# SwiGLU's splits one or two products later, operand reads two products later, and no idle reads at the end

## The chip, the cores and the metric

The kernel runs on one core of a Trainium2 chip. The metric is the device time of one execution in microseconds (us). A core has five engines that run side by side, each its own list of instructions in order: PE (TensorE, the matmuls; PEld is its weight load), DVE (VectorE), ACT (ScalarE), POOL (GpSimd) and SP (SyncE), which in this kernel does nothing but issue DMAs. The kernel is written with a manual schedule: the order of the Python calls is the order on each engine, and semaphores are put between them where one needs another's result.

## The reference

One layer with 512 tokens of width 2048: an input projection, three token mixers, an output projection, and a SwiGLU feed-forward with residuals. Only the last line of the layer matters here:

```python
    x = x + mix @ w_out[l]
    h2 = _rms_norm(x, norm2_g[l])
    x = x + (jax.nn.silu(h2 @ w_gate[l]) * (h2 @ w_up[l])) @ w_down[l]
```

The feed-forward's inner width is 5632, that is 44 blocks of 128. All is float32 and has to stay accurate, so each operand of a matmul is split in a high part (a cast to fp32r) and a low part (the rest), and three products of the parts are added.

## The kernel before, in words

**Stages.** From 0 to 585 us the projections and mixers (not touched). From 585 to 1436 us the gate and up products, in groups `Wide` g = 0 to 21. From 1436 us on the down products: `Turned` t = 0 to 7 up to 1754 us, then `Down` t = 8 to 15. In the program's main loop (L1594 on) the three are one loop over g, with t = g - 22, so that t = -2 and t = -1 are the last two groups of the gate and up stage.

**A group.** Each group multiplies two by two blocks by a Strassen scheme with seven products, in the order `ORDER = (5, 1, 7, 6, 2, 4, 3)`. The group's weights come as raw tiles of 128x1024 named '11', '12', '21', '22' with a group (w6, d0) and a sub-index 0 or 1. Sums of raw tiles (L213, POOL) make the other operands, tiles named 's'. One product of `Wide` and `Turned` is two units, one unit uses one weight tile and is 12 matmuls of 128x512 (L1387). So a group has 14 units. A unit's weight tile is first split: ACT casts it to `wn` (L277) and to `wh` (L278), DVE subtracts to `wl` (L279). `next_unit` writes the split of the tile that comes two units later (`SPLIT_AHEAD`), and there are three buffers of `wh` and `wl`. `pump` (L257 to L264) issues the read of the next raw tile on SP as soon as, in program order, its buffer is free.

**Operands of the gate and up products.** They are kept split, as tiles `h` named by product and block, in a pool of 68 slots. Those of products 1 and 7 (`KEEP`) stay; those of the other five are written to DRAM (`hd`) and read again (`load_op`, L1590) for the half of the blocks that the next odd group needs: two groups in a row share a half. These reads are queued in `loads`, three a product (`LOADS`), and each goes on SP at the end of the next product.

**SwiGLU's results.** An odd group g finishes the pair (g-1, g): its results go through Silu (L1524) to DRAM (`zd`). They come back as tiles of the two blocks p = g-1 and p = g, `f{p}r` and `f{p}l` (`Pair.load`, L1303), the r tiles one product after the group's last, the l tiles four products after. From them POOL makes sums `f{p}ta` and `f{p}tb` (`sums1`, `sums2`, L1311 to L1318), and four pieces are split into the seven operands `a{q}_{p}` of the down products: `piece3` from r, `piece4` from l, `piece1` from ta, `piece2` from tb. A piece is a near cast on ACT (L1323), one or two casts on ACT (L1330), one or two subtractions on DVE (L1331), and a write to DRAM (`od`, L1245) for each operand. `PIECES_AT` says how many products later each step runs, for p even and p odd, in the order sums1, sums2, piece3, piece4, piece1, piece2.

**Operands of the down products.** `load_act` (L1585) reads the tiles `a` back from `od`, four blocks for each product of t = 0.

**Queues.** `later(n, ..., queue=extras)` puts a call at the end of the n-th product from now; `run(extras)` runs what is due at the end of each product. All DMAs stand in SP's one list in this order, so a read that waits for a free buffer holds up all that stand behind it.

Of the kernel before, what the change touches and what calls it, by code (L numbers as in the profile page):

```python
# [70 lines left out]
ORDER = (5, 1, 7, 6, 2, 4, 3)  # L71
# [6 lines left out]
J_SET = NJ // 2  # L78


KEEP = (1, 7)
LOADS = 3
PIECES_AT = ((5, 5, 4, 5, 6, 7), (6, 6, 5, 6, 8, 11))


BY = 4
# [42 lines left out]
def kernel(ctx: ExitStack, tc: tile.TileContext, xT, wi, wo, wgu, wd, cst_in, outT):  # L129
# [34 lines left out]
    units = [wi[0][:, :T], wi[0][:, T:]] + [wi[u] for u in range(1, 2 * N_IN)]  # L164
# [3 lines left out]
    entries, works = [], []  # L168

    sums = defaultdict(list)  # L170
    raws, held = {}, {}

    def take(buf, key, n=1024):
        assert buf not in held
        held[buf] = key
        if buf[0] == "x":
            raws[key] = (wide(int(buf[1]), f"w{key}"), n)
        else:
            raws[key] = (wp.tile([P, 1024], F32, name=f"w{key}", tag=f"raw{buf}", bufs=1), n)
        return raws[key][0]  # L180

    def drop(key):
        for buf in [b for b, k in held.items() if k == key]:
            held.pop(buf)
        return raws.pop(key)

    for u, unit in enumerate(units):
# [9 lines left out]
    def down_group(name, n, subs):  # L197

        u, many = len(works), len(subs)
        key = {(k, i): (k, name, i) for k in ("11", "12", "21", "22", "s") for i in range(many)}  # L200
        into = {}
        for ks in (("21", "22"), ("11",), ("12",)):
            for i in range(many):
                for k in ks:
                    entries.append((ring(k if k[0] == "2" else "1"), key[k, i], subs[i][k]))
        for i in range(many):
            into[i] = ring("s")

        def add(i, to, a, b, last=None):
            def go():  # L210
                out = raws[key[to, i]][0] if to == a else take(into[i], key[to, i], n)
                eng = nc.vector if name == "w0" and "12" not in (a, b) else nc.gpsimd
                eng.tensor_add(out[:, :n], raws[key[a, i]][0][:, :n], raws[key[b, i]][0][:, :n])  # L213
                if last:
                    drop(key[last, i])
            return go

        for i in range(many):
            at_sum = FIRST_SUMS_AT[i] if name == "w0" else SUMS_AT[many][i]
            for d, args in zip(at_sum, (("s", "21", "22"), ("21", "21", "11"), ("s", "s", "11", "11"),  # L220
                                        ("s", "s", "12"))):
                sums[u + d].append(add(i, *args))
        for k, last in (("s", False), ("11", False), ("21", True), ("s", False), ("12", True), ("22", True), ("s", True)):
            works.extend((key[k, i], last, None) for i in range(many))
# [6 lines left out]
    def set_of(g):  # L231
        return (g + 1) // 2 % 2
# [20 lines left out]
    at = {"entry": 0, "split": 0, "use": 0}  # L253

    def pump(limit):
        while at["entry"] < len(entries) and len(raws) < limit and entries[at["entry"]][0] not in held:
            buf, key, parts = entries[at["entry"]]  # L257
            (part,) = parts
            n = part.shape[-1] * (part.shape[1] if len(part.shape) == 3 else 1)
            t = take(buf, key, n)[:, :n]  # L260
            nc.sync.dma_start(t if len(part.shape) == 2 else t.rearrange("p (n c) -> p n c", n=part.shape[1]), part)
            at["entry"] += 1
# [20 lines left out]
    def split_in_steps(i):  # L283

        def cast():
            if at["split"] > min(i, len(units) - 1):
                return
            u = at["split"]
            at["split"] += 1
            t, n = drop(works[u][0])  # L290
            hi = wp.tile([P, 1024], F32R, name=f"wh{u}", tag="hi", bufs=SPLIT_BUFS)
            lo = wp.tile([P, 1024], F32R, name=f"wl{u}", tag="lo", bufs=SPLIT_BUFS)
            nc.scalar.copy(hi, t)  # L293
            ticks.after(1, low, u, t, hi, lo)

        def low(u, t, hi, lo):
            nc.vector.tensor_sub(lo, t, hi.bitcast(F32))  # L297
            splits[u] = (hi, lo)

        ticks.after(1, cast)  # L300

    def sums_now():
        for fn in sums.pop(at["use"], ()):
            fn()

    def next_unit(ahead=SPLIT_AHEAD, split=split_up_to):
        sums_now()
        u = at["use"]
        at["use"] += 1
        split(u + ahead)  # L310
        pump(RAW_EARLY if u < 20 else RAW_BUFS + N_WIDE)
        return splits.pop(u)
# [724 lines left out]
    for name in PROJ[HEAD4:]:  # L1037
        kind, what, j = name[0], name[1], name[2:]
# [39 lines left out]
    ops, opening_ops = {}, {}  # L1078
# [160 lines left out]
    evacs, extras = [], []  # L1239
    flip = [1]  # L1240

    def run(queue):

        for fn, *args in queue.pop(0) if queue else ():
            fn(*args)  # L1245

    def later(n, fn, *args, queue=evacs):
        while len(queue) <= n:
            queue.append([])
        queue[n].append((fn, *args))  # L1250
# [103 lines left out]
    def load_y(t):  # L1354
        if N_TURNED <= t < N_DOWN:
            for n in (t - N_TURNED, t - N_TURNED + 8):
                y[n], x2[n] = slot(f"y{n}"), slot(f"x2_{n}")
                d = yd[n - n % 2]
                nc.sync.dma_start(y[n].rearrange("p (k a x) -> p k a x", k=2, a=4),
                                  bass.AP(tensor=d.tensor, offset=d.offset + n % 2 * P * 64,  # L1360
                                          ap=[[64, P], [P * T, 2], [32 * T, 4], [1, 64]]))
                nc.sync.dma_start(x2[n], x2d[n])
# [94 lines left out]
    class Wide(Turned):  # L1457
# [8 lines left out]
        def done(self, q, banks):  # L1466
# [38 lines left out]
            if q == 3:  # L1505
                for k, at in enumerate(PIECES_AT):
                    one = Pair(self.g - 1 + k)
# [84 lines left out]
    loads = []  # L1592
# [3 lines left out]
    for g in range(G_STEPS + N_DOWN):  # L1596
        t = g - G_STEPS
        turned = 0 <= t < N_TURNED
        if t < 0:
            blk = Wide(g, blk)  # L1600
        else:
            blk = (Turned if turned else Down)(t)
        for i, q in enumerate(ORDER):
            sums_now()
            run(evacs)
            for sub in range(BY // 2 if t < N_TURNED else 1):
                w = next_unit()
                if t < 0:
                    first = J_SET * set_of(g) + 2 * sub
                    blk.multiply(i, sub, w, [ops[q, j] for j in range(first, first + 2)])  # L1610
                    if ticks.due:
                        ticks.tick()
                elif turned:
                    first = BY * (t // 2) + 2 * sub
                    blk.multiply(i, sub, w, [acts[q, j] for j in range(first, first + 2)])
                else:
                    blk.multiply(q, w, [acts[q, j] for j in range(TURNED, NP)])
            if g == 0 and i in (2, 5):
                (norm2a if i == 2 else norm2b)()

            if t < 0 and (g % 2 == 0 or t == -1):
                for j in range(J_SET * set_of(g), J_SET * (set_of(g) + 1)):
                    if q not in KEEP or t >= -2:
                        ops.pop((q, j))
                        if 0 < g and t < -1:
                            loads.append((load_op, q, J_SET * (1 - set_of(g)) + j % J_SET))
                    if t == -1:
                        loads.append((load_act, q, [j % J_SET]))
                if g == 0 and i == 0:
                    held.pop("x1"), held.pop("x3")  # L1630
                    opening_ops.clear()
            elif turned and t % 2:
                first = BY * (t // 2)
                for j in range(first, first + BY):
                    acts.pop((q, j))
                first += BY
                if first < TURNED:
                    later(1, load_act, q, range(first, first + BY), queue=extras)
            for fn, *args in loads[:LOADS]:
                later(1, fn, *args, queue=extras)  # L1640
            del loads[:LOADS]
            if N_TURNED - 2 <= t < N_TURNED:
                n = 4 - (t % 2 == 0)
                for q2, j in rest[:n]:
                    later(1 if t % 2 else 0, load_act, q2, [j], queue=extras)
                del rest[:n]
            if i == (5 if turned else 3):
                load_y(t + 1)
            run(extras)
# [85 lines left out]
```

## Time and profile before

| what | us |
|---|---|
| median of 3 runs | 1877.76 (1877.58 to 1878.87) |
| profiled execution, device time | 1877.44 |
| its span, first to last instruction | 1875.2 |
| PE busy in the span | 1853.6 |
| DVE busy | 1533.1 |
| ACT busy | 1366.0 |
| POOL busy | 1082.9 |

By stage, from the view of busy time in stretches:

| stretch, us | PE | DVE | ACT | POOL | DMA share | GB/s |
|---|---|---|---|---|---|---|
| 0 to 585 | 583.11 | 479.30 | 301.06 | 221.49 | 0.46 | 147 |
| 585 to 1436 | 843.46 | 721.05 | 739.24 | 551.35 | 0.78 | 246 |
| 1436 to 1754 | 309.15 | 232.99 | 243.80 | 219.41 | 0.76 | 252 |
| 1754 to 1875 | 117.92 | 99.73 | 81.96 | 90.68 | 0.71 | 206 |

The page's other parts are: the span in 40 slices with PE's granted clock and the DMA load, the DMA queue (one queue of SP moves nearly everything, 398.89 of 400.60 MB), the chain of work that ended last (93% PE, 4% DMA, 1% ACT), the costliest groups of instructions, and the DMA issues, among them 208 reads of `h` (256 KB each, 5.4 us from issue to landing in the median), 154 writes of operands to `od` and 154 reads of them (5.8 us each). A row of the timeline has its start, its duration, engine, line, operation, output and inputs, and in brackets the engine's idle time ahead of it with what ended that.

### The profile page before, as it was taken

What the parts mean: (1) busy time and instruction counts of PE and PEld (TensorE: products, weight loads), DVE (VectorE), ACT (ScalarE), POOL (GpSimd) and SP (SyncE); (2) the same over time, 40 slices, a digit from 0 to 9 for tenths busy, and PEclk for the clock granted to TensorE, in tenths of its full rate; (3) what the DMA queues carried; (4) which work ended last, traced back from release to release, by engine and by line L of the source; (5) the groups of instructions that cost most, each with busy time, mean ns of one, the idle gap of its engine ahead of it and who ended that gap; (6) DMA issues with size and microseconds to landing.
All of it is one profiled execution on the core that took longest, in us unless ns stands there. A gap on an engine that the chain in (4) does not pass through costs nothing.

```text
span 1875.2 us, 26746 instructions
## 1 busy us (share of the span) xinstructions
PE 1853.6 (99%) x8548; PEld 1539.9 (82%) x8548; DVE 1533.1 (82%) x2318; ACT 1366.0 (73%) x1956; POOL 1082.9 (58%) x681
## 2 busy tenths in 40 slices
PE   9999999999999999999999999999999899999999
PEld 7888888888888888887888878888788688888888
DVE  7688899997579779798798887988878577778887
ACT  6235565555366789898898988988889787777675
POOL 5013444462253557576675676666766667766786
PEclk9999999999999999999999999999999899999999
DMA  7334333443397477879778797787889785578984
GB/s 260 135 100 120 99 98 98 117 129 111 118 326 243 128 201 243 265 235 291 227 238 271 230 297 235 234 271 225 286 258 323 229 306 190 192 256 286 308 238 124
DMA packets 319708, 400.60 MB, mean 214 GB/s; under 512 B 81104, under 2 KB 210256, under 8 KB 319568
## 3 DMA queue, kind: packets, MB, share of 16 engines
q1 hardware_dynamic: 319424, 398.89, 66.8%
q8 instruction: 68, 1.11, 0.3%
q14 instruction: 72, 0.59, 0.1%
q10 hardware_dynamic: 144, 0.01, 0.0%
HBM read 311.00 MB, written 80.22 MB: 209 GB/s over the span
## 4 chain that ended last, share of the span: by engine, by line
PE 93%; DMA 4%; ACT 1%; issue 1%; DVE 0%; SPq 0%; ACTq 0%; DVEq 0%
PE out L1387 56%; PE out L1279 6%; PE o L316 3%; PE o L315 3%; PE o L317 3%; PE cq L315 2%; PE cq L316 2%; PE cq L317 2%; PE in L316 1%; PE ak L315 1%; PE aq L315 1%; PE ak L317 1%; PE aq L317 1%; PE ak L316 1%; PE bu L316 1%; PE bu L315 1%
## 5 line engine op out<-in xcount | busy, mean ns | idle before, releaser
L1387 PE MATMUL out<-wh,h 128*128 128x512 f32 x2464 | 611.4, 390 | 7.5 <-ACT wh L278 7.3
L1387 PEld LDWEIGHTS out<-wh,h 128*128 128x128 f32 x2464 | 460.8, 188 | 109.5 <-ACT wh L278 13.9
L1387 PE MATMUL out<-wl,h 128*128 128x512 f32 x1232 | 329.3, 389 | 0.0
L1387 PEld LDWEIGHTS out<-wl,h 128*128 128x128 f32 x1232 | 231.3, 188 | 48.2
L1387 PE MATMUL out<-wh,a 128*128 128x512 f32 x896 | 225.0, 394 | 8.8 <-DMA a<-od 8.8
L1387 PEld LDWEIGHTS out<-wh,a 128*128 128x128 f32 x896 | 170.3, 190 | 45.2 <-DMA a<-od 5.3
L1387 PE MATMUL out<-wl,a 128*128 128x512 f32 x448 | 120.7, 392 | 0.0
L1387 PEld LDWEIGHTS out<-wl,a 128*128 128x128 f32 x448 | 85.0, 190 | 17.8
L517 DVE SCALAR_TENSOR_TENSOR y<-bu,cst,y 128x511 f32<-128x511 f32 (+14 forms) x120 | 94.5, 788 | 1.4
L1490 DVE TENSOR_TENSOR G<-G,out 128x512 f32<-128x512 f32 x132 | 83.6, 674 | 5.2 <-PE out L1387 5.2
L273 ACT CAST wh<-w 128x1024 fp32r<-128x1024 f32 (+1 forms) x41 | 42.1, 1032 | 56.4 <-PE o L316 34.3
L1279 PE MATMUL out<-a,wh 128*128 128x512 f32 x330 | 80.1, 391 | 0.0
L293 ACT CAST wh<-w 128x1024 fp32r<-128x1024 f32 x52 | 54.8, 1053 | 32.3 <-PE bg L316 9.2
L297 DVE TENSOR_TENSOR wl<-w,wh 128x1024 fp32r<-128x1024 f32 x52 | 65.3, 1256 | 14.3 <-ACT wh L293 14.2
L1487 DVE TENSOR_TENSOR G<-G,out 128x512 f32<-128x512 f32 x110 | 68.4, 677 | 1.7 <-PE out L1387 1.7
L1279 PEld LDWEIGHTS out<-a,wh 128*128 128x128 f32 x330 | 60.3, 188 | 11.4
L1528 DVE STREAM_TRANSPOSE z<-s 128x256 f32<-128x256 f32 x88 | 60.1, 682 | 3.0
L274 DVE TENSOR_TENSOR wl<-w,wh 128x1024 fp32r<-128x1024 f32 (+1 forms) x41 | 51.6, 1261 | 9.0 <-ACT wh L273 8.6
L315 PE MATMUL o<-mh_c,wh 128*128 128x512 f32 x128 | 51.2, 400 | 0.0
L317 PE MATMUL o<-mh_c,wl 128*128 128x512 f32 x128 | 50.1, 391 | 0.0
L316 PE MATMUL o<-ml_c,wh 128*128 128x512 f32 x128 | 49.9, 390 | 0.0
L1432 DVE TENSOR_TENSOR Y<-Y,out 128x512 f32<-128x512 f32 x48 | 30.8, 682 | 20.6 <-PE out L1387 20.4
(2758 smaller groups left out, 5121.5 us busy)
## 6 DMA issues: line engine op xcount, KB each, us to landing
h<-hd SPq DMA_DIRECT2D x208, 256.0 KB, 5.4
od<-a SPq DMA_DIRECT2D x154, 256.0 KB, 5.8
a<-od SPq DMA_DIRECT2D x154, 256.0 KB, 5.8
w<-in_wi SPq DMA_DIRECT2D x59, 512.0 KB, 3.5
w<-in_wo SPq DMA_DIRECT2D x32, 512.0 KB, 3.5
hd<-h SPq DMA_DIRECT2D x56, 256.0 KB, 4.9
zd<-z SPq DMA_DIRECT2D x44, 256.0 KB, 4.7
x<-in_xT SPq DMA_DIRECT2D x16, 256.0 KB, 6.9
```

The source lines that it names most:

```text
L274: eng.tensor_sub(lo[:, :n], t[:, :n], hi[:, :n].bitcast(F32))
L293: nc.scalar.copy(hi, t)
L297: nc.vector.tensor_sub(lo, t, hi.bitcast(F32))
L315: nc.tensor.matmul(out, wh, xh, start=start, stop=False)
L316: nc.tensor.matmul(out, wh, xl, start=False, stop=False)
L317: nc.tensor.matmul(out, wl, xh, start=False, stop=stop)
L517: nc.vector.scalar_tensor_tensor(yconv[j][:, i:], hconv[j][:, :T - i], c, yconv[j][:, i:], op0=ALU.mult, op1=ALU.add)
L1279: nc.tensor.matmul(out, lhs[:, s], rhs, start=begin, stop=last and low == flip[0] and x is xs[-1], skip_group_check=True)
L1387: nc.tensor.matmul(to[h], x[:, h * P:(h + 1) * P], v[:, j], start=sub == 0 and h not in started, stop=sub == 1 and n in (len(todo) - 1, le ...
L1487: op(t, t, b)
L1490: nc.vector.tensor_add(t, t, b)
L1528: nc.vector.transpose(to[:, :, h], s[:, cols].rearrange("p (c b) -> p b c", b=8))
```

## The change

1. `PIECES_AT`: for the even block of a pair `sums1` and `sums2` run 6 products after the group's last one instead of 5, `piece4` (the l tile) at 7 instead of 5, `piece1` at 7 instead of 6, `piece2` at 8 instead of 7. For the odd block the sums run at 7 instead of 6, `piece4` at 11 instead of 6, `piece1` at 10 instead of 8. `piece3` stays at 4 (even) and 5 (odd), and `piece2` of the odd block stays at 11.
2. The reads of `h` for groups before t = -2 go on SP two products later than before (`later(3, ...)` for `later(1, ...)`).
3. `pump` refills a raw buffer one unit later than it could by program order (`LAG = 1`), in the stages after the projections.
4. At t = -2 the tiles of products 1 and 7 are no longer read again (eight reads of 256 KB that nothing used). The reads of `a` for t = 0 are queued two products ahead of their own product instead of with it, the first two products' at the end of t = -2, and from t = -2 on four reads a product go out instead of three.

```diff
-PIECES_AT = ((5, 5, 4, 5, 6, 7), (6, 6, 5, 6, 8, 11))
+PIECES_AT = ((6, 6, 4, 7, 7, 8), (7, 7, 5, 11, 10, 11))
+LAG = 1
...
-    raws, held = {}, {}
+    raws, held, freed = {}, {}, {}
...
             held.pop(buf)
+            freed[buf] = at["use"]
...
-        while at["entry"] < len(entries) and len(raws) < limit and entries[at["entry"]][0] not in held:
+        while at["entry"] < len(entries) and len(raws) < limit:
             buf, key, parts = entries[at["entry"]]
+            if buf in held or at["use"] > len(units) and freed.get(buf, 0) + LAG > at["use"]:
+                break
...
             if t < 0 and (g % 2 == 0 or t == -1):
-                for j in range(J_SET * set_of(g), J_SET * (set_of(g) + 1)):
+                for j in range(J_SET):
                     if q not in KEEP or t >= -2:
-                        ops.pop((q, j))
-                        if 0 < g and t < -1:
-                            loads.append((load_op, q, J_SET * (1 - set_of(g)) + j % J_SET))
-                    if t == -1:
-                        loads.append((load_act, q, [j % J_SET]))
+                        ops.pop((q, J_SET * set_of(g) + j))
+                    if q not in KEEP and 0 < g and t < -1:
+                        loads.append((load_op, q, J_SET * (1 - set_of(g)) + j))
+                    if t == -1 and i < len(ORDER) - len(KEEP):
+                        loads.append((load_act, ORDER[i + len(KEEP)], [j]))
+                if t == -2 and i == len(ORDER) - 1:
+                    loads.extend((load_act, ORDER[n], [j]) for n in range(len(KEEP)) for j in range(J_SET))
...
-            for fn, *args in loads[:LOADS]:
-                later(1, fn, *args, queue=extras)
-            del loads[:LOADS]
+            n = LOADS + (t >= -2)
+            for fn, *args in loads[:n]:
+                later(3 if t < -2 else 1, fn, *args, queue=extras)
+            del loads[:n]
```

PE's list is the same instruction for instruction. SP's has 1214 instead of 1222 rows. What moves, at the three places that the prediction speaks of:

ACT, where group 7 begins (`w7` are group 7's weight tiles; the pair of blocks 4 and 5 is on its way back). Before:

```order
L1323 CAST f4n_8405<-f4l 128x256
L1330 CAST a_4_8407<-f4l 128x4x2x32
L1323 CAST f5n_8410<-f5r 128x512
L1330 CAST a_5_8412<-f5r 128x4x2x32
L1330 CAST a_5_8415<-f5r 128x4x2x32
L277 CAST wn_8431<-w('s', 'w7', 0)_8321 128x1024
L278 CAST wh_8429<-w('s', 'w7', 0)_8321 128x1024
```

The same place on ACT with the change (lines from here on have shifted by four):

```order
L1327 CAST f5n_8393<-f5r 128x512
L1334 CAST a_5_8395<-f5r 128x4x2x32
L1334 CAST a_5_8398<-f5r 128x4x2x32
L281 CAST wn_8408<-w('s', 'w7', 0)_8311 128x1024
L282 CAST wh_8406<-w('s', 'w7', 0)_8311 128x1024
L281 CAST wn_8427<-w('s', 'w7', 1)_8373 128x1024
L282 CAST wh_8425<-w('s', 'w7', 1)_8373 128x1024
L281 CAST wn_8463<-w('11', 'w7', 0)_8321 128x1024
L282 CAST wh_8461<-w('11', 'w7', 0)_8321 128x1024
L281 CAST wn_8482<-w('11', 'w7', 1)_8323 128x1024
L282 CAST wh_8480<-w('11', 'w7', 1)_8323 128x1024
L1327 CAST f4n_8500<-f4l 128x256
```

The piece of `f4l` (its near cast and its cast for one operand), which stood ahead of group 7's first weight split, now stands behind the splits of four of that group's tiles (eight casts).

SP, in the middle of group 7, where the last operand tiles of that group are read (`h3_0` to `h3_3`, used by its last product; `w8` is the next group's weights). Before:

```order
L261 DMA w('21', 'w8', 1)_8587<-in_wgu 128x4x256
L1590 DMA h3_0_8609<-hd0_3889 128x512
L1590 DMA h3_1_8611<-hd1_3890 128x512
L1590 DMA h3_2_8613<-hd2_3891 128x512
L1245 DMA od4_5833<-a6_4_8539 128x512
L1245 DMA od4_5833<-a4_4_8542 128x512
L1590 DMA h3_3_8658<-hd3_3892 128x512
L1245 DMA od5_5834<-a5_5_8603 128x512
L1245 DMA od5_5834<-a7_5_8606 128x512
L261 DMA w('22', 'w8', 1)_8713<-in_wgu 128x4x256
```

With the change:

```order
L1249 DMA od4_5833<-a4_4_8575 128x512
L1594 DMA h3_0_8687<-hd0_3889 128x512
L1594 DMA h3_1_8689<-hd1_3890 128x512
L1594 DMA h3_2_8691<-hd2_3891 128x512
L265 DMA w('22', 'w8', 1)_8723<-in_wgu 128x4x256
L265 DMA w('11', 'w8', 0)_8725<-in_wgu 128x4x256
L265 DMA w('11', 'w8', 1)_8727<-in_wgu 128x4x256
L265 DMA w('12', 'w8', 0)_8729<-in_wgu 128x4x256
L1594 DMA h3_3_8756<-hd3_3892 128x512
L1249 DMA od5_5834<-a5_5_8681 128x512
```

The read of `h3_3` stood ahead of the four weight tiles of the next group and now stands behind them.

SP, at the end of the gate and up stage (`d0`, `d1` are the weights of t = 0 and t = 1, `a6_2` is the operand of product 6 and block 2). Before:

```order
L1245 DMA zd21_1_13979<-z21_11_14363 128x512
L261 DMA w('21', 'd1', 0)_14450<-in_wd 128x4x256
L261 DMA w('22', 'd1', 0)_14452<-in_wd 128x4x256
L261 DMA w('21', 'd1', 1)_14472<-in_wd 128x4x256
L1303 DMA f20r_14495<-zd21_1_13979 128x8x64
L1303 DMA f21r_14497<-zd21_1_13979 128x8x64
L1585 DMA a6_2_14499<-od2_5831 128x512
L1585 DMA a6_3_14501<-od3_5832 128x512
```

With the change:

```order
L265 DMA w('22', 'd0', 1)_14223<-in_wd 128x4x256
L265 DMA w('11', 'd0', 0)_14225<-in_wd 128x4x256
L265 DMA w('11', 'd0', 1)_14227<-in_wd 128x4x256
L265 DMA w('12', 'd0', 0)_14229<-in_wd 128x4x256
L1589 DMA a6_0_14256<-od0_5829 128x512
L1589 DMA a6_1_14258<-od1_5830 128x512
L1589 DMA a6_2_14260<-od2_5831 128x512
L1589 DMA a6_3_14262<-od3_5832 128x512
```

The operands of product 6 were read behind three weight tiles of t = 1 and the r tiles of the last pair; now they are read behind t = 0's own weight tiles.

## The prediction

> **What bounds the kernel now.** I read the page's first part, then PE's waits, then the timeline around each kind of wait, then the chain of work behind it.
>
> ```profile
> span 1875.2 us, 26746 instructions
> ...
> PE 1853.6 (99%) x8548; PEld 1539.9 (82%) x8548; DVE 1533.1 (82%) x2318; ACT 1366.0 (73%) x1956; POOL 1082.9 (58%) x681
> ```
>
> PE is busy for all but 1875.2 - 1853.6 = 21.6 us, and its list does not change. So the change can only take away idle time of PE and matmuls that run slowly, or add some. PE's waits, from the view that sums them:
>
> ```profile
> PE out L1387 <- DMA a<-od: 8.8, 2, 4.9
> PE out L1387 <- ACT wh L278: 7.3, 9, 1.5
> ```
>
> Two waits of 8.8 us in all for operands of the down products, and nine of at most 1.5 us for a weight's high part. The unit without a wait is the measure, here from the down stage (start, duration):
>
> ```profile
> 1525.97 1.98 PE L1387 MATMUL out<-wh,a 128*128 128x512 f32 x8
> ...
> 1528.69 1.98 PE L1387 MATMUL out<-wh,a 128*128 128x512 f32 x8
> ```
>
> One unit is 1528.69 - 1525.97 = 2.72 us, so a pair of groups of 28 units is 76.16 us. Now the first and the last of the short stalls, and one in the middle with its neighbours:
>
> ```profile
> 701.75 2.12 PE L1387 MATMUL out<-wh,h 128*128 128x512 f32 x8 [0.46 <-ACT wh L278]
> ...
> 852.67 1.98 PE L1387 MATMUL out<-wh,h 128*128 128x512 f32 x8
> ...
> 856.91 2.12 PE L1387 MATMUL out<-wh,h 128*128 128x512 f32 x8 [1.36 <-ACT wh L278]
> ...
> 859.78 1.98 PE L1387 MATMUL out<-wh,h 128*128 128x512 f32 x8
> ...
> 1397.84 2.11 PE L1387 MATMUL out<-wh,h 128*128 128x512 f32 x8 [0.87 <-ACT wh L278]
> ```
>
> From 701.75 to 1397.84 there are 696.09 us, and nine pairs should take 9 x 76.16 = 685.44: 10.65 us are lost between these two rows. In the middle one 856.91 - 852.67 - 2.72 = 1.52 us go ahead of the unit and 859.78 - 856.91 - 2.72 = 0.15 in it. It lies where an odd group begins, ten times in all. Why there, ACT's timeline of that place shows:
>
> ```profile
> 846.52 1.06 ACT L278 CAST wh<-w('s', 'w6', 1)_8001 128x1024 fp32r<-128x1024 f32 x1 [0.26 <-PE out L1387]
> 853.11 0.38 ACT L1323 CAST f4n<-f4l 128x256 fp32r<-128x256 f32 x1 [5.53 <-DMA f4l<-zd]
> ...
> 853.73 0.58 ACT L1323 CAST f5n<-f5r 128x512 fp32r<-128x512 f32 x1
> ...
> 854.87 1.01 ACT L277 CAST wn<-w('s', 'w7', 0)_8321 128x1024 fp32r<-128x1024 f32 x1
> 855.81 1.04 ACT L278 CAST wh<-w('s', 'w7', 0)_8321 128x1024 fp32r<-128x1024 f32 x1
> 856.76 1.01 ACT L277 CAST wn<-w('s', 'w7', 1)_8379 128x1024 fp32r<-128x1024 f32 x1
> ...
> 858.66 0.58 ACT L1323 CAST f4n<-f4ta 128x512 fp32r<-128x512 f32 x1
> ```
>
> ACT stands 5.53 us in front of the piece of f4l, and behind it wait the piece of f5r and the split of group 7's first weight, which PE needs. The chain of work has the reason, and the line of that read (L1303) its spread:
>
> ```profile
> 843.50 9.54 DMA f4l<-zd
> ```
>
> ```profile
> DMA to landing us min/median/max: 5.6/7.9/9.7
> ```
>
> The read is issued at 843.50, and ACT's turn comes at about 847.6, before 853.04. The other loss is where the down stage begins:
>
> ```profile
> 1452.50 1.98 PE L1387 MATMUL out<-wh,a 128*128 128x512 f32 x8
> ...
> 1459.35 3.53 PE L1387 MATMUL out<-wh,a 128*128 128x512 f32 x8 [3.97 <-DMA a<-od]
> ...
> 1477.85 2.07 PE L1387 MATMUL out<-wh,a 128*128 128x512 f32 x4 [4.87 <-DMA a<-od]
> ...
> 1490.61 1.75 PE L1387 MATMUL out<-wh,a 128*128 128x512 f32 x7
> ```
>
> From 1452.50 to 1490.61 there are 38.11 us for nine units, which are 24.48: 13.63 lost, of which 3.97 + 4.87 = 8.84 are the gaps and 4.79 slow matmuls behind them (3.53 us for eight that otherwise take 1.98). The clock's column says why, in the view of stretches (PE, PEld, DVE, ACT, POOL, then granted clock, DMA share, GB/s):
>
> ```profile
> 1397.00:1435.00 38.00, 37.16 (x163) 30.62 (x164) 34.80 (x49) 34.62 (x46) 28.14 (x18) 1.00 0.95 321
> ...
> 1459.35:1463.75 4.40, 4.40 (x13) 3.50 (x13) 0.26 (x1) 1.13 (x2) 0.00 (x0) 0.61 0.99 357
> ```
>
> The granted clock was 0.61 behind the 3.97 us gap. [...]
>
> **The change, part by part.** Sums are made against the profiled execution, 1877.44 us (span 1875.2 and 2.24 around it); the median of the runs shown is 0.3 higher.
>
> *The l piece two products later.* It now stands behind the splits of four weights of the odd group. The fourth can only begin when PE has finished the group's first unit, at 852.67 + 2 x 2.72 = 858.1, so ACT comes to f4l about 859, 6 us after it landed; at the longest landing of 9.7 us still. The ten stalls go. The nine pairs give 10.65, the first stall adds its 0.46 and some 0.15 of slow matmuls: 11.3 as an upper end. A few tenths are single slow matmuls elsewhere in the pairs, which stay; I take **10.9**. What is next on ACT: two splits take 858.66 - 854.87 = 3.79 us of a product's 5.44, so 1.65 are free. At step 7 there now stand the f4l piece (853.73 - 853.11 = 0.62) and the ta piece (854.87 - 853.73 = 1.14 for one of the same shapes), 1.76: 0.11 over, once a pair, against three buffers. At nothing; if ACT has no lead there, it costs between 0 and 1.76 a pair. The sums on POOL go one product later with the piece that reads them, and keep their distance. The odd block's pieces go to steps 10 and 11: their writes are read much later (its own blocks' turn is in the down stage), at nothing, except behind the last pair, where both pieces fall into t = 1: from 0 to 1.76 us there, I take 0, because the down stage's unit rows above run at 2.72 with ACT doing the same splits.
>
> *The operand reads two products later.* Their number and their bytes stay. The tightest is `h3_3`, which now stands behind four weight tiles. The rows of SP and of DVE there, the landing of the last of them, the PE row that needs it, and the spread of all h reads (L1590):
>
> ```profile
> 872.46 0.64 SPq L261 DMA_DIRECT2D w('21', 'w8', 1)_8587<-in_wgu  x1
> ...
> 876.73 0.32 SPq L1590 DMA_DIRECT2D h<-hd  x1
> ...
> 882.58 0.38 SPq L261 DMA_DIRECT2D w('22', 'w8', 1)_8713<-in_wgu  x1
> ...
> 885.79 1.68 SPq L1245 DMA_DIRECT2D od<-a  x2
> ```
>
> ```profile
> 881.31 1.21 DVE L279 TENSOR_TENSOR wl<-w('22', 'w7', 0)_8148,wn 128x1024 fp32r<-128x1024 f32 x1
> ```
>
> ```profile
> od<-a SPq DMA_DIRECT2D x1, 256.0 KB, 7.7
> ```
>
> ```profile
> 892.50 1.98 PE L1387 MATMUL out<-wh,h 128*128 128x512 f32 x8
> ```
>
> ```profile
> DMA to landing us min/median/max: 3.2/5.4/8.8
> ```
>
> Before, SP issued h3_3 at 876.73 and stood then for DVE's wl, done at 882.52, before the four weights. The first write behind them was issued at 885.79 and landed 7.7 later, at 893.5. That is the place h3_3 gets. PE needs it as the second operand of its unit, four matmuls behind 892.50, at 893.4. So with DVE as late as here it is 0.1 us late, nine times (groups 3 to 19): 0.9. With the longest landing of 8.8 it is 1.2 late: 10.8. But DVE's split here runs behind ACT, which had lost 1.5 us at the group's start and no longer does, so it should come some tenths to 1.5 us earlier against PE. I take **0.5** in all, between nothing and the nearest row, and keep 0 and 10.8 for the range. The other reads of h have a product or more of room, by the same rows: h3_0 to h3_2 are no longer ahead of any wait of SP.
>
> *The refill one unit later.* It moves one tile, ('21', 1), past the reads of r and writes of results. It was issued at 872.46, its partner in the sum, ('22', 1), at 882.58: 10.1 us to spare against one unit of 2.72. At nothing; without that spare it would cost up to 2.72 us in a group.
>
> *The end.* The SP rows around the transition:
>
> ```profile
> 1427.29 0.76 SPq L261 DMA_DIRECT2D w('12', 'd0', 0)_14213<-in_wd  x1
> ...
> 1452.35 4.86 SPq L1585 DMA_DIRECT2D a<-od  x3
> ...
> 1468.63 3.57 SPq L1303 DMA_DIRECT2D f21l<-zd  x1
> 1472.26 4.36 SPq L1585 DMA_DIRECT2D a<-od  x5
> ```
>
> The read that PE missed at 1459.35 (a6_2) was the first issued in the row 1452.35, and that missed at 1477.85 (a4_3) the first in the row 1472.26, behind f21l. Now product 6's reads stand right behind the weight that was issued at 1427.29, about 20 us earlier, and product 4's two products earlier too, ahead of f20l and f21l. Cost: what the queue then has to carry. The reads of a after 1435 (L1585, its row for 1435:1480), and the reads of h in 1397:1435:
>
> ```profile
> L1585 SPq DMA_DIRECT2D a<-od x20: 319/390/3907, 1436.6 to 1476.2; - x20
> ```
>
> ```profile
> h<-hd SPq DMA_DIRECT2D x13, 256.0 KB, 5.6
> ```
>
> In 1397:1435 the queue moved 321 GB/s x 38 us = 12.2 MB. At most the 20 reads of 0.262 MB move in, +5.2. Ahead of this stretch eight idle reads go, so about eight of its 13 h reads come before it, -2.1: an estimate of 15.3 MB. At the 357 GB/s of the row 1459.35 that takes 42.9 us, 4.9 more than the 38 there are. The a6 reads, behind 1427.29 at four of 0.262 MB and a landing of 8.8, arrive at about 1440, and PE asks for them at 1459.35 - 3.97 = 1455.4: 15 us in hand for 4.9. So all **13.6** go. The idle reads are worth nothing by themselves, since nobody waits for them.
>
> [...]
>
> Sum: 10.9 + 13.6 - 0.5 = 24.0, so 1877.44 - 24.0 = 1853.4 and 0.3 for the median: **1853.7 us**.
>
> **The rivals.**
>
> *h3_3 late, or ACT short.* For it: 0.1 us late by the nearest row, and ACT 0.11 over its room at step 7. Against it: both were measured with ACT 1.5 us behind. It gives 1 to 10.8 us back: 1855 to 1864.
>
> *The end stays bound.* Reads issued earlier queue behind a load of 0.95 share, and an a tile still comes late. If the clock stays low as well, all 13.6 are kept: 1853.7 + 13.6 = 1867.3; with a wait of 1 to 3 us, 1855 to 1857. Against it: 15 us in hand for 4.9.
>
> *The change doesn't do what it says at the short stalls.* ACT finds the next late tile (ta, which POOL makes from l and r) and PE stalls a product later by the same 10.9: 1864.6. Against it: the l tile landed at 853.0, and ta is read only after 859.
>
> *Slower.* The one mechanism is h3_3 behind the weights, if DVE's wl of ('22', 0) comes a whole unit later than now, because its subtractions of the moved pieces now fall in that group. Then h3_3 lands at 896.2, 2.8 us late, nine times 25.2, 1.2 more than is gained: 1878.9. The point from which it decides is 24.5 / 9 = 2.7 us late in each odd group. With 8.8 to landing it is 3.9 late, as long as the gap that had the low clock, with 3.53 - 1.98 = 1.55 of slow matmuls behind it: 9 x 5.45 = 49, near 1902. Against it: DVE is busy 34.80 of 38 us in the row 1397, and the pieces moved are 0.4 to 0.7 us each, a fifth of what it takes.
>
> **How the numbers follow.** All gone with remainders up to 1.5 us: 0.70, 1852.5 to 1855. h3_3 late or ACT short: 0.14. The end still bound: 0.05. The short stalls moved: 0.04. No net gain, by h3_3 at about its breaking point: 0.03. Slower: 0.04. The predicted time is the first's. The range takes it and most of the second and part of the third: 1851.8 (the 11.3 instead of 10.9, no remainder, and 0.6 for the spread of the runs, 1877.58 to 1878.87) to 1863. A measurement of this kernel can tell about 0.2%, 3.8 us, from no change: faster is below 1874.0, slower above 1881.5. Faster 0.93, same 0.03, slower 0.04.
>
> **What the profile of the changed kernel would show.** Right: PE's waits have neither line any more, PE idle under 3 us in the span; nine pairs between the first units of odd groups take 685.5 to 687; ACT comes to f4l without a wait; granted clock 1.00 from 1436 on. Wrong: PE rows with a wait on `DMA h<-hd` in the last product of odd groups (h3_3), on ACT's wh in the middle of odd groups (step 7), or on `DMA a<-od` with 0.5 to 0.6 of the clock behind it. What would break the forecast most is the landing of h3_3 behind four weights, a row measured once.

## The result and the profile after

The changed kernel takes 1851.77 us (median of 4 runs, 1851.51 to 1852.13), the kernel before 1877.99 (4 runs, 1877.58 to 1878.87): 26.2 us less, a ratio of 0.986 with a 95% interval of 0.9843 to 0.9877. The forecast was 1853.7 with a range of 1851.8 to 1863.0, so the time lies 0.03 us below the range: the mechanisms forecast are there, the gain is 2 us larger than their sum.

The page of the changed kernel, first lines (span; busy time of each engine):

```profile
span 1849.7 us, 26751 instructions
...
PE 1844.3 (100%) x8548; PEld 1538.4 (83%) x8548; DVE 1533.8 (83%) x2318; ACT 1370.2 (74%) x1956; POOL 1083.0 (59%) x681
```

PE's idle time in the span went from 21.6 to 1849.7 - 1844.3 = 5.4 us, and its busy time by 9.3 us, which are matmuls that no longer run slowly. PE's waits, summed, in the changed kernel:

```profile
PE idle L417 <- DVE bones L350: 1.4, 1, 1.4
PE a2o L880 <- DVE a2pl L866: 0.3, 1, 0.3
PE in L320 <- DVE wl L278: 0.2, 1, 0.2
```

All three lie in the first stage. Both lines of before, the 8.8 us for a and the 7.3 us for wh, are gone. By stage (stretch, its length, busy time of PE, PEld, DVE, ACT, POOL, then granted clock, DMA share, GB/s):

```profile
585.00:1436.00 851.00, 850.89 (x3757) 704.14 (x3756) 732.25 (x998) 755.84 (x990) 561.12 (x323) 1.00 0.79 252
1436.00:1754.00 318.00, 318.00 (x1438) 264.69 (x1437) 246.04 (x311) 249.67 (x288) 229.79 (x131) 1.00 0.76 254
```

PE was busy for 843.46 and 309.15 us in the same stretches before. Now ACT's timeline at the start of group 7, the place of the prediction:

```profile
849.76 1.05 ACT L282 CAST wh<-w('s', 'w7', 1)_8373 128x1024 fp32r<-128x1024 f32 x1 [0.24 <-PE out L1391]
850.71 1.01 ACT L281 CAST wn<-w('11', 'w7', 0)_8321 128x1024 fp32r<-128x1024 f32 x1
852.48 1.05 ACT L282 CAST wh<-w('11', 'w7', 0)_8321 128x1024 fp32r<-128x1024 f32 x1 [0.75 <-PE out L1391]
...
855.25 1.05 ACT L282 CAST wh<-w('11', 'w7', 1)_8323 128x1024 fp32r<-128x1024 f32 x1 [0.81 <-PE out L1391]
856.21 0.37 ACT L1327 CAST f4n<-f4l 128x256 fp32r<-128x256 f32 x1
```

ACT has no wait in front of f4l any more. Its waits here are for PE, which still holds the buffers: ACT is as far ahead as three buffers let it be.

To compare runs I use PE's loss in a stage: the time between the starts of the stage's first unit and of the next stage's, less 2.7195 us for each of the 308 units of gate and up and 2.72 for each of the 112 of t = 0 to 7. For gate and up that is the distance of these rows, changed kernel, less 308 units (837.6 us):

```profile
585.03 1.98 PE L1391 MATMUL out<-wh,h 128*128 128x512 f32 x8
...
1424.38 1.98 PE L1391 MATMUL out<-wh,a 128*128 128x512 f32 x8
```

839.35 - 837.6 = 1.75 us lost: 1.6 in group 0, whose start the change does not touch, and the rest because the unit measures 2.7200 from group 1 on. Before, the same rows stand at 585.30 and 1436.18: 13.27 lost. So the short stalls gave 11.52 us. In t = 0 to 7 of the down stage 13.63 were lost before, and 0.0 now.

### The profile page after: what moved, and what is told of

Same layout as the page of the kernel before. It is cut to its first block, busy times and chain, and to the rows that moved or that the text cites. A ratio compares the mean times of both kernels' runs of the same rounds, so it can differ in the third digit from the quotient of the medians.

```text
span 1849.7 us, 26751 instructions
## 1 busy us (share of the span) xinstructions
PE 1844.3 (100%) x8548; PEld 1538.4 (83%) x8548; DVE 1533.8 (83%) x2318; ACT 1370.2 (74%) x1956; POOL 1083.0 (59%) x681
## 4 chain that ended last, share of the span: by engine, by line
PE 99%; ACT 0%; DVE 0%; DMA 0%; issue 0%; SPq 0%; ACTq 0%; DVEq 0%
PE out L1391 62%; PE out L1283 6%; PE o L321 3%; PE o L319 3%; PE o L320 3%; PE cq L319 2%; PE cq L320 2%; PE cq L321 2%; PE in L320 1%; PE aq L319 1%; PE ak L319 1%; PE ak L321 1%; PE aq L321 1%; PE bu L320 1%; PE ak L320 1%; PE bu L321 1%
## 5 line engine op out<-in xcount | busy, mean ns | idle before, releaser
L1391 PE MATMUL out<-wh,a 128*128 128x512 f32 x896 | 221.3, 389 | 0.0
L301 DVE TENSOR_TENSOR wl<-w,wh 128x1024 fp32r<-128x1024 f32 x52 | 65.3, 1256 | 14.3 <-ACT wh L297 14.0
```

The costliest lines, as they stand in the source:

```text
L1391: nc.tensor.matmul(to[h], x[:, h * P:(h + 1) * P], v[:, j], start=sub == 0 and h not in started, stop=sub == 1 and n in (len(todo) - 1, le ...
```

## The experiments

The first four take parts of the change alone. The table gives all runs; the loss columns are from each run's own profiled execution. For a kernel with short stalls one execution tells the gate and up column only roughly: before, p2, p3 and p6 have the same short stalls (what p2, p3 and p6 change lies behind group 19), and they lost between 11.3 and 14.7.

| kernel | median us | loss, gate and up | loss, down stage |
|---|---|---|---|
| before | 1877.99 | 13.3 | 13.6 |
| changed | 1851.77 | 1.8 | 0.0 |
| p1: new PIECES_AT alone | 1862.45 | 1.8 | 9.7 |
| p2: edits of the end alone | 1868.42 | 12.1 | 6.4 |
| p3: idle reads dropped alone | 1868.32 | 11.3 | 6.5 |
| p6: four reads a product alone | 1870.88 | 14.7 | 5.6 |
| p13: l piece of the even block at 7, alone | 1867.94 | 2.7 | 15.0 |
| c3: l piece at 7 and four reads | 1863.85 | 3.6 | 9.0 |
| d3: even block's steps and the end | 1853.73 | 1.8 | 1.4 |
| d2: PIECES_AT and idle reads dropped | 1854.66 | 1.8 | 1.9 |
| d1: PIECES_AT and four reads | 1852.31 | 1.8 | 0.0 |
| d4: d1 and idle reads dropped | 1852.31 | 1.8 | 0.0 |
| c1: PIECES_AT and all edits of the end | 1852.15 | 1.8 | 0.0 |
| p8: changed, operand reads three products later | 1873.83 | 28.1 | 0.0 |

### p1, the pieces alone

```diff
-PIECES_AT = ((5, 5, 4, 5, 6, 7), (6, 6, 5, 6, 8, 11))
+PIECES_AT = ((6, 6, 4, 7, 7, 8), (7, 7, 5, 11, 10, 11))
```

> Before with the new PIECES_AT alone. Theory (ACT's place alone makes the short stalls): the ten stalls go, 11.5 us, and the 13.6 at the start of the down stage stay: 1866.4, between 1865.9 and 1867. Rival (the later operand reads or the later refills are needed as well, because they let the l tile land sooner): ACT still waits for l and half or more of the 11.5 stays: 1872 or above.

Measured 1862.45 (1862.14 to 1862.79), ratio 0.9917 (0.9902 to 0.9932): 4 us better than expected. The loss in gate and up is that of the whole change, so the later operand reads and refills are not needed for it, and the rival falls. The down stage lost 9.7 instead of 13.6, with the reads of a where they were. PE's rows there:

```profile
1445.96 2.08 PE L1387 MATMUL out<-wh,a 128*128 128x512 f32 x8 [1.51 <-DMA a<-od]
...
1463.07 2.07 PE L1387 MATMUL out<-wh,a 128*128 128x512 f32 x4 [5.06 <-DMA a<-od]
```

The first wait is 1.51 instead of 3.97, and eight matmuls behind it take 2.08 instead of 3.53. The pieces' move thus reaches into the next stage: the read of a6_2 went out 14.4 us behind the start of t = 0 instead of 16.2. SP issues in step with DVE's releases of weight buffers (in 1400:1460 it stood 6.2 us for `wl` in the kernel before), and that these no longer run late is the likely reason; it was not tried by itself.

### p2, the end alone

The edits of the last two blocks of the diff, with `later(1, ...)` for all reads; PIECES_AT, operand reads and refills as before.

> Before with the edits of the end alone (idle reads gone, reads of a queued two products ahead, four a product). Theory: the two waits for a and their slow matmuls go, 13.6 us, the ten short stalls stay: 1864.3, between 1863.8 and 1865. Rival (the queue is full there, and the moved reads are late elsewhere): at least one wait for a stays, 1867 or above.

Measured 1868.42 (1868.29 to 1868.64), ratio 0.9949 (0.9934 to 0.9963): 4 us worse than expected. No wait for a is left, but there are four new stalls of 0.5 to 1.3 us for ACT. ACT's waits in 1425:1500 of this run:

```profile
ACT wn L277 <- POOL w('s', 'd0', 1)_14289 L213: 5.3, 1, 5.3
ACT f20n L1323 <- DMA f20l<-zd: 4.3, 1, 4.3
```

The second is the eleventh of the l waits, that of the last pair; in the kernel before it lay under the wait for a. The first was 2.3 us before. POOL waits for the weight ('22', 'd0', 1), and SP's rows have it behind twelve of the moved reads:

```profile
1413.52 2.76 SPq L1585 DMA_DIRECT2D a<-od  x4
...
1419.09 3.16 SPq L1585 DMA_DIRECT2D a<-od  x4
...
1423.84 3.10 SPq L1585 DMA_DIRECT2D a<-od  x4
1427.31 0.38 SPq L261 DMA_DIRECT2D w('22', 'd0', 1)_14211<-in_wd  x1
```

This run's t = 0 starts at 1435.10, so the weight is issued 7.8 us ahead of it. The changed kernel has the same reads ahead of it, and issues it 12.4 us ahead:

```profile
1411.97 0.38 SPq L265 DMA_DIRECT2D w('22', 'd0', 1)_14223<-in_wd  x1
```

So what held it up was not the packing alone, but packing on top of an SP that follows a late ACT, DVE and POOL (c1 below has the packing with the new pieces, and issues the weight 12.7 us ahead). The rival (a wait for a stays) falls, but the queue did make something else late.

### p3, the idle reads alone

```diff
-                        if 0 < g and t < -1:
+                        if q not in KEEP and 0 < g and t < -1:
```

> Before without the eight idle reads, nothing else: three reads a product, each product's reads of a queued with their own product. The prediction's claim: worth nothing, 1877.8. Rival: the list of loads is a backlog, and eight reads less let the reads of a go out one product earlier, ahead of the weights of t = 1 and of the r tiles for a6_2, ahead of the l tiles for a4_3; then most of 13.6 goes with this alone, 1864.3 to 1866 (a2_1 now stands where a6_2 stood and may be a few tenths late).

Measured 1868.32 (1867.19 to 1870.64), ratio 0.995 (0.9935 to 0.9964). The prediction's claim that the idle reads are worth nothing falls: ten microseconds go with this one condition, 7.2 of them in the down stage by the profiled executions; the 2.0 in gate and up are mostly the scatter of the short stalls. The rival has the mechanism right; its time, 1866 at most, was 2 us too low. Nobody waits for these reads, but all others wait behind them in the list `loads`, which lets three out a product. What is left is a read that took a4_3's place behind the l tiles, a3_2:

```profile
1465.46 2.83 SPq L1303 DMA_DIRECT2D f21l<-zd  x1
1468.39 3.06 SPq L1585 DMA_DIRECT2D a<-od  x2
```

```profile
1474.29 3.39 PE L1387 MATMUL out<-wh,a 128*128 128x512 f32 x8 [3.63 <-DMA a<-od]
```

### p6, four reads a product alone

```diff
-            for fn, *args in loads[:LOADS]:
+            n = LOADS + (t >= -2)
+            for fn, *args in loads[:n]:
                 later(1, fn, *args, queue=extras)
-            del loads[:LOADS]
+            del loads[:n]
```

> Before with four reads a product from t = -2 on, nothing else: the idle reads stay and nothing is queued earlier. SP's order at the start of the down stage is then that of the whole change. Theory (the pace of the list of loads makes the two waits, not the product with which a read is queued): all 13.6 go, 1864.3. Rival (the reads have to be queued two products ahead): the waits stay, 1877.8; with the idle reads in the queue as well it could be slower by the time of eight reads, up to 5 us.

Measured 1870.88 (1868.93 to 1874.88), ratio 0.9964 (0.9953 to 0.9976). The waits for a are gone with this alone, as the theory says, but the time is not 1864.3, for the reason found in p2: ACT waited 5.2 us for the sum of ('s', 'd0', 1) and 3.6 for f20l, and the down stage lost 5.6. Queueing the reads two products ahead was not run by itself: alone, it leaves the order of the reads as it was, since the list `loads` already has seven reads waiting where t = -1 begins.

### p8, the slower rival by force

```diff
-                later(3 if t < -2 else 1, fn, *args, queue=extras)
+                later(4 if t < -2 else 1, fn, *args, queue=extras)
```

> The changed kernel with the operand reads three products later than before instead of two: h3_0 to h3_2 now stand behind the four weights as well. [...]

Measured 1873.83 (1870.74 to 1878.25), ratio to before 0.9975 (0.9964 to 0.9986), 22 us more than the changed kernel; its profiled execution, 1877.81, lost 26.4 us more than that of the changed kernel. My estimate ahead of it came from the changed kernel's rows, which are shown below: there the read behind the four weights landed 8.5 us after its issue and 1.1 us ahead of its use; h3_0 in its place is used 3.6 us earlier, so 2.6 us late, in nine odd groups, 1851.8 + 9 x 2.6 to 3 = 1875 to 1879, with no slow matmuls. The profiled execution lies in that, by two errors against each other, and the median 1 us below: PE waited once in each of the nine odd groups, 1.5 to 3.5 us and 19.5 in all from start to start (18.0 of it idle, by the view of waits) where 23 to 27 were expected, and some 6.7 us more were slow matmuls, where none were expected (the last section). So the forecast's slower rival is real, one product away, though even here the median stays 4 us below the kernel before: two products later is the last step that costs nothing. In the changed kernel the landing of h3_3 (the read of L1594 issued at 879.85) and its use were:

```profile
DMA to landing us min/median/max: 8.5/8.5/8.5
```

```profile
888.54 1.98 PE L1391 MATMUL out<-wh,h 128*128 128x512 f32 x8
```

It landed at 888.39 and was used four matmuls behind 888.54, at 889.45: 1.06 us to spare.

### c1 and p13: both halves, and one number

c1 is p1 and p2 together, with the operand reads and refills of before.

> Before with the new PIECES_AT and the edits of the end, but operand reads one product ahead as before and refills without the lag. Theory (the two halves need each other: the pieces give ACT, DVE and with them SP their lead, without which the moved reads of a hold up the weight ('22', 'd0', 1); the later operand reads and the lag carry nothing): 1851.8, between 1851.3 and 1852.5. Rival (the later operand reads and the lag are what keeps the weight early): some of the 6.4 us of loss in t = 0 and 1 that the end's edits alone left stays, 1853 to 1858.

Measured 1852.15 (1851.71 to 1852.47), ratio 0.986 (0.9845 to 0.9875): the whole gain. The later operand reads and the lag carry nothing that shows in the time or in the losses, and the halves need each other: alone they gain 15.5 and 9.6 us against the 1877.99 above, and what looks like a sum is each half removing part of the other's loss in t = 0.

```diff
-PIECES_AT = ((5, 5, 4, 5, 6, 7), (6, 6, 5, 6, 8, 11))
+PIECES_AT = ((5, 5, 4, 7, 6, 7), (6, 6, 5, 6, 8, 11))
```

> Before with one number changed: the even block's l piece at 7 products instead of 5. Theory (this piece in front of the odd group's first split is the whole cause of the short stalls): the stage of gate and up loses 1.8 us of PE as with the full PIECES_AT, and the start of the down stage the 9.7 it lost there: 1862.4, within 0.7. Rival (the ta piece at 6, which stands for POOL's sums, which stand for l, takes its place): ACT waits for f4ta and PE stalls a unit later, 1866 or above.

Measured 1867.94 (1867.39 to 1868.79), ratio 0.9945 (0.993 to 0.9959). Neither is right. The short stalls go with this one number (loss 2.7 in gate and up), although ACT does now wait for f4ta, as the rival has it; its lead takes it up. But the down stage lost 15.0, more than before, with waits for a of 4.18 and 4.72 us that both have slow matmuls behind them (eight in 2.81 us, where 1.98 is usual, and one in 0.79, where 0.39 is).

### c3, d3: why the sums had to move too

c3 is p13 with p6; d3 is the end's edits with the new steps of the even block alone, `((6, 6, 4, 7, 7, 8), (6, 6, 5, 6, 8, 11))`.

> Before with two numbers changed: the even block's l piece at 7 products instead of 5, and four reads a product from t = -2 on; idle reads, operand reads, sums and the other pieces as before. Theory (ACT's lead and the pace of the list of loads are all): 1851.8, up to 1853 if the eight idle reads still crowd the queue. Rival (the other pieces or the idle reads matter): waits of ACT or PE of 2 us or more in t = 0 and 1, 1854 or above.

Measured 1863.85 (1863.03 to 1865.56), ratio 0.9925 (0.9909 to 0.9942): 11 us above the theory. POOL's waits of this run in 1380:1440 show why:

```profile
POOL w('s', 'd0', 1)_14305 L213 <- DMA w('22', 'd0', 1)_14227<-in_wd: 9.4, 1, 9.4
POOL w('s', 'w21', 1)_13871 L213 <- DVE a L1331: 8.6, 1, 8.6
POOL f18ta L1311 <- DMA f18l<-zd: 4.7, 1, 4.7
```

With the sums still at step 5, POOL itself stands 4.7 us for f18l, ahead of the weight sums that ACT needs (3.3 us in the kernel before, which has three reads less to carry ahead of that weight). From there POOL has no break up to its sum for ('s', 'w21', 0), which ends at 1401.57, and SP stands for that sum before it can refill the raw buffer:

```profile
1399.16 2.41 POOL L213 TENSOR_TENSOR w('s', 'w21', 0)_13811<-w('s', 'w21', 0)_13811,w('11', 'w21', 0)_13793 128x1024 f32<-128x1024 f32 x1
```

```profile
SPq L261 <- POOL w('s', 'w21', 0)_13811 L213: 5.8, 1, 5.8
```

All that SP carries behind it gets late, and the weight ('22', 'd0', 1) is issued at 1423.28, 3.6 us ahead of t = 0 at 1426.92 instead of 12.4. PE then stalled for 4.12 us. The l tile is waited for at two places, on ACT and on POOL, and it is the second that decides how much SP can carry at the end.

> Before with the edits of the end and the new steps for the even block alone (sums at 6, l piece and ta piece at 7, tb piece at 8); the odd block's steps as before. Theory (what stands for f4l and for the sums of it is what costs, and those are the even block's): 1852.1, up to 1853. Rival (the odd block's l piece at 6, ahead of the even block's, or two pieces at step 8 take ACT's lead): PE stalls on wh in odd groups or in t = 0 and 1, 1854 or above.

Measured 1853.73 (1853.08 to 1854.14), ratio 0.9872 (0.9857 to 0.9887), 10 us better than c3, and without POOL's wait for f18l. d3 also lacks the idle reads that c3 has; d1 below keeps them, with the new steps, and loses nothing. So nearly all is the even block's steps. The odd block's steps carry the last 1.4 us: with them as before ACT waits 1.1 us for f5l at the start of group 7, 3.8 us for the sum of ('s', 'd0', 1), and PE 0.5 us for wh in t = 0. The rival is right by that much.

### d1, d4, d2: what of the end's edits is needed

d1 is p1 with p6, the idle reads still there. d4 is d1 without the idle reads. d2 is p1 with p3.

> Before with the new PIECES_AT and four reads a product from t = -2 on; the eight idle reads stay and nothing is queued earlier. Theory (with ACT's lead there, the pace alone is enough at the end): 1852.1, up to 1853. Rival (the idle reads, 2.1 MB in the fullest stretch, make the weight ('22', 'd0', 1) late again): 1854 or above, with ACT waiting for POOL's sum of it.

> Before with the new PIECES_AT, without the idle reads and with four reads a product, but each product's reads of a queued with their own product, not two ahead. Theory (the two products ahead carry nothing, since there is no backlog left): 1852.1 within 0.6, as with all edits of the end. Rival (reads nearer to their use fall behind t = 0's own weights and come late): a wait for a of over 1 us, 1854 or above; or, the other way, fewer reads ahead of the weight ('22', 'd0', 1) and a time under 1851.5.

Both measured 1852.31 (1851.71 to 1854.20, and 1852.06 to 1854.17), ratios 0.9866 and 0.9867 (0.9852 to 0.9881 each), and lost nothing in the down stage. So PIECES_AT and the pace of four give all of the gain; with them the idle reads are worth nothing that these runs can tell. The two products ahead are worth nothing at all: at four reads a product without the idle reads the same reads leave the list at the same products with and without them, and SP's reads and writes in the traces of d4 and c1 stand in the same order.

> Before with the new PIECES_AT and without the idle reads; three reads a product as before. Theory (with eight reads less in the list, a3_2 and no longer a4_3 is the first behind the l tiles, and it is used a product later): it lands 0 to 1.7 us late, 1852 to 1854, the clock stays up. [...]

Measured 1854.66 (1853.68 to 1855.53), ratio 0.9879 (0.9862 to 0.9895). a3_2 is 1.6 us late, once, and the matmuls behind it keep their pace, as expected; the median is 0.7 above the expected span.

```profile
PE out L1387 <- DMA a<-od: 1.6, 1, 1.6
```

No run beat the changed kernel: PE has no idle time left in the stages that the change touches.

## Why the prediction was right or wrong

**What was mis-sized.** The profiled executions differ by 1877.44 - 1851.51 = 25.93 us, and the sum said 24.0. By terms:

| term | forecast | measured |
|---|---|---|
| short stalls | 10.9 | 11.5 |
| start of the down stage | 13.6 | 13.6 |
| h3_3 late | -0.5 | 0.0 |
| stages that the change does not touch | 0 | 0.3 |
| around the span | 0 | 2.24 - 1.81 = 0.4 |

The mechanisms came as forecast; the step that failed is the size of three terms of the sum.

The first is the short stalls, 11.5 instead of 10.9. From an upper end of 11.3 the forecast took off 0.4 for single slow matmuls that were thought to be apart from the stalls and to stay. They went too: they stood in the first units behind each stall, and from their first unit on the odd groups lost 2.5 us before and nothing after. That ACT had lost its lead there and weights were ready just in time is the likely reason. The other 0.2 are the slow matmuls of the last odd group, which lie behind the row at 1397.84 where the forecast stopped counting.

The second is the 0.5 for h3_3, which cost nothing. The third is what the change does not touch, put at nothing, which differed by 0.7 between the two executions. It is scatter: over the 14 profiled executions here the time around the span is 1.7 to 2.2 us, with the one of before at the upper end, and PE's busy time in 0:585 is 582.8 to 583.2; the first unit of gate and up starts at 585.30 before and at 585.03 with the change.

That the time misses the range by only 0.03 us is owed to a slip: the low end does not follow from its parts, which give 1877.44 - 11.3 - 13.6 + 0.3 - 0.6 = 1852.2 and not 1851.8. By its parts the low end was 0.4 us too high, less than the scatter that it left out.

**The l piece.** Right, with the place, the cause and the number of stalls. ACT was expected at f4l 6 us after its landing, with 0.11 us a product too little; the trace shows waits for PE there and none for f4l, so there was room at step 7. Its size holds for this one execution: less group 0, the same stalls make 9.5 to 12.9 us in the four executions that have them.

**The sums on POOL** were put at nothing, because they keep their distance to the piece. Wrong as a reason: POOL stood for the same l tile (3.95 us for f4l in the kernel before), and c3 against d3 shows 10 us for the even block's sums, ta and tb steps once four reads a product go out. It cost the forecast nothing, since the change moves both.

**The operand reads and the refill.** Right: nothing gained (c1), and h3_3 tight. It had 1.06 us at group 7, where the nearest row had said -0.1 and the reason given (DVE no longer late) some tenths to 1.5 more. p8 shows the slower rival's price.

**The end.** Right in size, wrong in its parts. It was put down to reads queued two products ahead, but that alone changes no instruction's place; it is the pace of the list, and by itself even dropping the idle reads, which the prediction had at nothing (p3: 10 us). And the 13.6 us are not the end's own: with the reads on time and the pieces as before, 6.4 us of ACT stalls come out from under them (p2). The rival "the end stays bound" named the full queue; it has that effect, on a weight and not on a tile of a, and only while SP runs late. The 357 GB/s that the prediction took for the queue's pace were not its limit here: the changed kernel moved 375 GB/s over the same stretch, 14.3 MB where 15.3 were estimated (stretch, length, busy time of PE, PEld, DVE, ACT, POOL, then granted clock, DMA share, GB/s):

```profile
1397.00:1435.00 38.00, 38.00 (x169) 31.49 (x168) 33.73 (x48) 34.15 (x46) 26.62 (x14) 1.00 1.06 375
```

**The clock behind a short wait.** The rival "the end stays bound" adds a wait of 1 to 3 us with nothing for slow matmuls behind it (1855 to 1857). No run shows that for the whole of 1 to 3 us: behind p1's gap of 1.51 us the granted clock was 1.00 (1445.60:1451.00), but behind two of p8's, 1.88 and 2.29 us, it was 0.73 (813:817) and 0.50 (1210.8:1214), as the last section shows.

## What to carry to other kernels

A read that nobody waits for still costs if the reads behind it in a paced list are waited for (p3, about 10 us): look at what the list holds back, not at who uses the read. When a late tile is read on two engines, moving its use on one of them can leave the wait standing on the other (c3 against d3, 10 us); find every reader of it, and what each has queued behind it. And a long wait can lie over shorter ones (p2, 6.4 us under 13.6): take the parts of a change alone before crediting a part with what the profile shows at its place.

## What was not expected of the hardware

**The clock fell behind gaps of 1.88 and 2.29 us, and not behind one of 2.14.** Two of p8's waits, and a third of a length between them (start, duration, gap in brackets):

```profile
813.40 2.52 PE L1391 MATMUL out<-wh,h 128*128 128x512 f32 x8 [1.88 <-DMA h<-hd]
815.71 1.91 PE L1391 MATMUL out<-wl,h 128*128 128x512 f32 x4
```

```profile
1210.94 3.58 PE L1391 MATMUL out<-wh,h 128*128 128x512 f32 x8 [2.29 <-DMA h<-hd]
```

```profile
1054.16 2.08 PE L1391 MATMUL out<-wh,h 128*128 128x512 f32 x8 [2.14 <-DMA h<-hd]
1056.08 1.07 PE L1391 MATMUL out<-wl,h 128*128 128x512 f32 x4
```

With the granted clock in the stretches around the three:

```profile
813.00:817.00 4.00, 3.60 (x12) 2.91 (x13) 2.23 (x3) 1.55 (x3) 4.00 (x3) 0.73 1.05 402
```

```profile
1210.80:1214.00 3.20, 3.06 (x7) 2.48 (x8) 1.54 (x2) 0.00 (x0) 3.20 (x2) 0.50 1.05 404
```

```profile
1054.00:1058.00 4.00, 3.84 (x17) 3.22 (x18) 2.49 (x4) 1.71 (x4) 4.00 (x2) 1.00 1.05 403
```

Behind 1.88 and 2.29 us the clock fell for a while, to 0.73 and 0.50 in these stretches (1.7 and 1.6 us lost), and behind 2.14 it stayed at 1.00. Behind each of the eight gaps of 3.5 us or more that the runs' rows show, matmuls were slow: behind 3.50, 3.97, 4.87 and 5.06 us the clock was 0.50, 0.61, 0.50 and 0.50; behind 3.63, 4.12 and 4.18 eight matmuls took 3.39, 3.78 and 2.81 us instead of 1.98; and behind 4.72 one took 0.79 instead of 0.39. What decides between 1.9 and 2.3 us was not tried, and no run shows it.

**Some kernels spread more than others.** The kernel before ran between 1874.72 and 1883.73 in the 30 runs beside these experiments, and p8, with its nine waits, between 1870.74 and 1878.25 in ten; the four kernels without PE waits (changed, c1, d1, d4) between 1851.51 and 1854.20, four runs each. That the waits make the spread is not shown: p1 and p2, which have waits too, stayed within 0.65 and 0.35 us in four runs each.
